# Small pads that move the start addresses of TensorE's operands, in a hybrid decoder block on one core

## The chip, the cores and the metric

The kernel runs on one core of one Trainium2 chip. A core has a matrix engine (TensorE, PE in the profile, which reads two operands from the on-chip memory SBUF: the moving one, streamed through the array, and the stationary one, the weights, which a separate load puts into the array), VectorE (DVE), ScalarE (ACT), GpSimd (POOL) and a queue engine (SP) that issues most transfers. SBUF has 128 partitions; a tile takes the same range of bytes in each of them, and a start address here is the byte in that range. The metric is device microseconds (us) of one execution, lower is better, as the median of several runs.

## The reference

One decoder layer over 512 tokens of width 2048, all in float32:

```python
mod = jax.nn.silu(c) @ w_ada[l] + b_ada[l]
sh1, sc1, ga1, sh2, sc2, ga2 = jnp.split(mod, 6, axis=-1)
h = modulate(rmsnorm(x, g_mix_norm[l]), sh1, sc1)
proj = h @ w_in[l]
...
y_ssm = s5_mixer(u, ...)            # diagonal complex state space, 64 groups of 16 channels
y_att = nsa_mixer(q, kc, vc, ks, vs, kw, vw, gl, ...)   # 16 heads, 4 key/value heads
y = jnp.concatenate([rmsnorm(y_ssm, g_ssm_out[l]), rmsnorm(y_att, g_nsa_out[l])], axis=-1) @ w_out[l]
x = x + ga1[:, None, :] * y
h = modulate(rmsnorm(x, g_ffn_norm[l]), sh2, sc2)
x = x + ga2[:, None, :] * conv_ffn(h, w_up[l], conv_w[l], conv_b[l], w_down[l])
return rmsnorm(x, g_final)
```

`conv_ffn` multiplies by `w_up` (2048 x 11264), runs a causal convolution of width 3 over each channel, gates one half with the silu of the other and multiplies by `w_down` (5632 x 2048).

## The kernel before, in words

Every large product keeps float32 precision by three passes (`mm3`, lines 87 to 89): each operand is split into a high part (a cast, on ACT) and a low part (the rest, a subtraction on DVE; both on line 62), and the product is hi x hi, then hi x lo, then lo x hi, summed in one PSUM tile. In the names, `wh` and `wl` are high and low part of a piece of weights and `ah`/`al`, `yh`/`yl`, `hh`/`hl`, `b11h`/`b11l` those of the activations. The three matmuls of a step thus alternate between two moving operands and two stationary ones. In a name of the trace such as `dn<-ah,wh`, `dn` is the result, `ah` the moving operand and `wh` the stationary one.

The program runs in stages, each with its pools of tiles:

- `phase_a` and `phase_b1` (to about 520 us): the input projections (results `b` and `mm`, operands `hh`, `hl`, 512 columns) and the state-space part `s5_octet`, in 8 octets.
- `phase_b2` (to about 860 us): attention, with the gated unit `glu` and half of the output projection as filler (`mm<-yh`).
- `phase_c` (to about 975 us): the other half of the output projection (`mm<-yh` again), with the modulation weights `wada` streamed in.
- `up_first` and `up_rest` (to about 1875 us): the product with `w_up`. `up_first` does two columns of tiles plainly, `up_rest` the other 42 (`c` = 2 to 43) by Strassen's scheme in Winograd's form: seven products of 24 matmuls of 256 columns each per `c` (8 steps of `mm3`), each with its own moving operand, in this order on PE: `b11`, `t4`, `b21`, `t1`, `t2`, `b22`, `t3` (a part of `t4` stands ahead of `b21`, the rest behind it). The weights of the products alternate between two pairs of tiles by a counter over all products (`turn`): `wh`, `wl` of the pool `wp`, and `xh`, `xl` of the pool `pe`. Seven is odd, so a product that reads `wh` in one `c` reads `xh` in the next one.
- `down` (to the end): the product with `w_down` (result `dn`, moving `ah`, `al`, stationary `wh`, `wl`, 512 columns; the last quarter in halves of 256, partly from a further weight tile `wz`), then the final norm.

Pools take SBUF from two ends: a pool is stacked on the left or, with `side="right"`, on the right, in steps of 32 bytes, and a tile's start follows from the sizes of everything below it in its stack. `cp` (small vectors and constants) and then `wp` (the weights' buffers `wr`, `wh`, `wl`) are at the bottom on the left for the whole program. Above them come the pools of the stages; `ta` (the taps of the convolution) goes in after `phase_b1` and stays. On the right stand `sc` (a vector `silc`), `pg` (`yh`, `yl`, `yatt`, `z`), later `pt` (the operands `b11` to `t3` of `up_rest`), later `pr` (`ah`, `al`).

Of the kernel before, what the change touches and what calls it, by code (L numbers as in the profile page):

```python
# [10 lines left out]
F32 = mybir.dt.float32  # L11
# [7 lines left out]
P = 128  # L19
# [5 lines left out]
NFF = D_FF // P  # L25
# [14 lines left out]
NV = 168  # L40

C_ID, C_T31, C_INVD, C_INVH, C_INVH4, C_SGN, C_NSGN, C_GRP, C_CHN, C_COS, C_SIN = (
    0, 192, 193, 194, 195, 196, 197, 198, 206, 334, 846)
# [8 lines left out]
class Block:  # L52
# [88 lines left out]
    def setup(self):  # L141
        nc, tc, a, ctx = self.nc, self.tc, self.a, self.ctx
        self.cp = ctx.enter_context(tc.tile_pool(name="cp", bufs=1))
        self.wp = ctx.enter_context(tc.tile_pool(name="wp", bufs=1))
        self.dp = ctx.enter_context(tc.tile_pool(name="dp", bufs=1, space=DRAM))
        cp = self.cp
        self.vecs = cp.tile([P, NV], F32, name="vecs")
        self.cons = cp.tile([P, C_COS], F32, name="cons")
        self.ident = self.cons[:, C_ID:C_ID + P]
        self.mhalf = cp.tile([P, 1], F32, name="mhalf")  # L150
        nc.vector.memset(self.mhalf, -0.5)
        self.mod = cp.tile([P, 6, KT], F32, name="mod")
        self.mad = cp.tile([P, 6, KT], F32, name="mad")
        d = self.dp

        self.u_d = d.tile([8, 8, P, 64], F32, name="u_d")

        self.z_d = d.tile([8, P, 8, 64], F32, name="z_d")

        self.k_s = d.tile([8, 16, 15 * P], F32, name="k_s")  # L160

        self.qk_d = d.tile([3, HD * 8, 2, S], F32, name="qk_d")

        self.c_d = d.tile([2, 2 * P, S], F32, name="c_d")
        self.sh_d = d.tile([1, D], F32, name="sh_d")
        self.x_d = d.tile([P, KT, S], F32, name="x_d")
        self.x2_d = d.tile([P, KT, S], F32, name="x2_d")

        self.a_d = d.tile([P, NFF, S], F32, name="a_d")
        self.v_d = d.tile([4, P, S], F32, name="v_d")  # L170
# [319 lines left out]
    def s5_octet(self, o, Tb, W, ps):  # L490
# [3 lines left out]
        G = slice(g0, g0 + 8)  # L494
        hp = self.tc.high_priority
        U, bc = self.s5_next
        SS = W.tile([P, 8, 65], F32, name="s5SS")
        V.memset(SS[:, :, 0:1], 0.0)
        bx, cx = bc[:, 0], bc[:, 1]

# [124 lines left out]
        V.tensor_mul(z5, z3, Sf)  # L625
        V.tensor_add(SS[:, :, 1:65], z4.rearrange("p (g j) -> p g j", g=8), z5.rearrange("p (g j) -> p g j", g=8))
        with hp():
            Y = ps.tile([P, S], F32, name="acc", bufs=4)
            for g in range(8):
                T.matmul(Y[:, 64 * g:64 * g + 64], w3[:, :, g], U[:, g], start=True, stop=False)  # L630
                T.matmul(Y[:, 64 * g:64 * g + 64], TT[:, g, 0:8].rearrange("p k h -> p (k h)"), SS[:, g, 0:64],
                         start=False, stop=True)
# [677 lines left out]
    def run(self):  # L1310
        tc = self.tc
        self.setup()
        sc = ExitStack()
        self.silc = sc.enter_context(tc.tile_pool(name="sc", bufs=1, side="right")).tile([P, D], F32, name="silc")
        lt = ExitStack()
        with tc.tile_pool(name="ph", bufs=1) as ph:
            hh, hl = map(list, zip(*[[ph.tile([P, S], F32R, name=f"h{x}{k}") for x in "hl"] for k in range(KT)]))
            with tc.tile_pool(name="psa", bufs=1, space=PSUM) as ps:
                self.phase_a(hh, hl, ph, ps)
            self.late(lt.enter_context(tc.tile_pool(name="pk", bufs=1, reuse_waits="tile", side="right")))  # L1320
            self.phase_b1(hh, hl)
        ta = self.ctx.enter_context(tc.tile_pool(name="ta", bufs=1, reuse_waits="tile"))
        self.taps = ta.tile([P, 88, 4], F32, name="taps")
        self.tapn = ta.tile([P, NFF, 3], F32, name="tapn")
        with ExitStack() as st:
            with ExitStack() as sg:
                pg = self.pg = sg.enter_context(tc.tile_pool(name="pg", bufs=1, reuse_waits="tile", side="right"))
                ps = sg.enter_context(tc.tile_pool(name="psd", bufs=1, reuse_waits="tile", space=PSUM))
                self.acc_att = pg.tile([P, S], F32, name="acc_att")
                self.acc_ssm = pg.tile([P, S], F32, name="acc_ssm")  # L1330
                self.rba = [pg.tile([P, 256], F32, name=f"rba{i}") for i in range(2)]
                yatt = pg.tile([P, 8, S], F32, name="yatt")
                yh = pg.tile([P, 8, S], F32R, name="yh")
                yl = pg.tile([P, 8, S], F32R, name="yl")
                self.phase_b2(yatt, yh, yl, ps)
                px = st.enter_context(tc.tile_pool(name="px", bufs=1, reuse_waits="tile"))
                x2 = [px.tile([P, 4, S], F32, name=f"x2{q}") for q in range(4)]
                self.acc2 = px.tile([P, S], F32, name="acc2")
                self.rb2 = px.tile([P, S], F32, name="rb2")
                W = st.enter_context(tc.tile_pool(name="py", bufs=1, reuse_waits="tile"))  # L1340
                with tc.tile_pool(name="pz", bufs=1, reuse_waits="tile") as Wa:
                    self.phase_c(x2, yatt, yh, yl, W, Wa, ps)
            lt.close()
            sc.close()
            self.phase_d(x2, W, st)
# [143 lines left out]
```

## Time and profile before

| | us |
|---|---|
| median of three runs | 2400.34 |
| the three runs | 2392.76, 2400.34, 2401.52 |
| the profiled execution, whole | 2398.66 |
| its span, first to last instruction | 2396.9 |
| PE busy in it | 2244.6 (94%) |
| DVE busy | 1865.8 (78%) |
| ACT busy | 1084.3 (45%) |

The span is 1.8 us shorter than the profiled execution's own time, which is 1.7 us under the median. Busy is the time in which at least one instruction of the engine was under way. Matmuls overlap: one that takes 0.28 us from its start to its end may be followed by the next 0.11 us after its start. How fast PE works is therefore read from the distance between starts of matmuls in the timeline, not from busy time or durations.

### The profile page before, as it was taken

What the parts mean: (1) busy time and instruction counts of PE and PEld (TensorE: products, weight loads), DVE (VectorE), ACT (ScalarE), POOL (GpSimd) and SP (SyncE); (2) the same over time, 40 slices, a digit from 0 to 9 for tenths busy, and PEclk for the clock granted to TensorE, in tenths of its full rate; (3) what the DMA queues carried; (4) which work ended last, traced back from release to release, by engine and by line L of the source; (5) the groups of instructions that cost most, each with busy time, mean ns of one, the idle gap of its engine ahead of it and who ended that gap; (6) DMA issues with size and microseconds to landing.
All of it is one profiled execution on the core that took longest, in us unless ns stands there. A gap on an engine that the chain in (4) does not pass through costs nothing.

```text
span 2396.9 us, 34691 instructions
## 1 busy us (share of the span) xinstructions
PE 2244.6 (94%) x13694; PEld 1967.3 (82%) x13694; DVE 1865.8 (78%) x2776; ACT 1084.3 (45%) x1807; POOL 288.5 (12%) x375
## 2 busy tenths in 40 slices
PE   7778999989899879899999999999999899999997
PEld 5666787866677667889999999999999788888887
DVE  7789877749988878889999999999999685433436
ACT  3322444448867742644444444444444322221215
POOL 7996110100000011000000000000000000000000
PEclk9989998979999889999999999999999999999999
DMA  9666744676576567233333333333332684323223
GB/s 339 255 223 215 235 146 140 186 207 195 174 233 218 186 251 289 101 120 119 119 119 119 119 119 119 120 119 119 119 119 102 243 322 182 139 90 126 101 88 106
DMA packets 92370, 398.17 MB, mean 166 GB/s; under 512 B 19776, under 2 KB 28352, under 8 KB 56240
## 3 DMA queue, kind: packets, MB, share of 16 engines
q1 hardware_dynamic: 77856, 344.60, 41.6%
q0 software_dynamic: 14352, 51.36, 6.1%
q8 instruction: 107, 1.75, 0.3%
q14 instruction: 55, 0.45, 0.1%
HBM read 358.20 MB, written 37.69 MB: 165 GB/s over the span
## 4 chain that ended last, share of the span: by engine, by line
PE 71%; DVE 11%; issue 6%; POOL 5%; ACT 4%; DMA 3%; SPq 0%; POOLq 0%; DVEq 0%; ACTq 0%
PE dn L88 7%; PE dn L87 7%; PE dn L89 7%; PE sa L89 7%; PE sa L87 7%; PE sa L88 7%; PE sb L87 5%; PE sb L89 5%; PE sb L88 5%; PE mm L87 2%; PE mm L89 2%; PE mm L88 2%; DVE wl L62 2%; DVE adw L111 1%; PE s L870 1%
## 5 line engine op out<-in xcount | busy, mean ns | idle before, releaser
L62 ACT CAST wh<-wr 128x1024 fp32r<-128x1024 f32 (+1 forms) x257 | 261.9, 1024 | 519.7 <-PE dn L88 331.6
L62 DVE TENSOR_TENSOR wl<-wr,wh 128x1024 fp32r<-128x1024 f32 (+1 forms) x255 | 307.2, 1209 | 68.6 <-ACT wh L62 47.7
L87 PE MATMUL dn<-ah,wh 128*128 128x512 f32 (+1 forms) x704 | 274.9, 391 | 7.6 <-ACT ah L62 7.6
L88 PE MATMUL dn<-al,wh 128*128 128x512 f32 (+1 forms) x704 | 278.0, 395 | 0.0
L89 PE MATMUL dn<-ah,wl 128*128 128x512 f32 (+1 forms) x704 | 273.3, 388 | 0.0
L1249 DVE SCALAR_TENSOR_TENSOR x<-dn,mod,x 128x512 f32<-128x512 f32 (+1 forms) x104 | 73.2, 707 | 203.4 <-PE dn L89 202.8
L87 PEld LDWEIGHTS dn<-ah,wh 128*128 128x128 f32 x704 | 132.8, 189 | 40.8 <-ACT ah L62 7.8
L89 PEld LDWEIGHTS dn<-ah,wl 128*128 128x128 f32 x704 | 132.7, 189 | 30.3
L111 DVE SCALAR_TENSOR_TENSOR adw<-adw,silc 128x2048 f32<-128x2048 f32 x63 | 147.9, 2348 | 12.1 <-DMA adw<-in_wada_dram 11.8
L88 PEld LDWEIGHTS dn<-al,wh 128*128 128x128 f32 x704 | 132.8, 189 | 29.6 <-DVE al L62 0.4
L87 PE MATMUL mm<-yh,wh 128*128 128x512 f32 (+1 forms) x320 | 130.4, 412 | 22.5 <-DVE x L1026 7.2
L62 ACT CAST wh<-wq 128x1024 fp32r<-128x1024 f32 x84 | 88.0, 1048 | 137.6 <-DVE wq L1193 101.0
L62 ACT CAST xh<-wq 128x1024 fp32r<-128x1024 f32 x84 | 88.5, 1054 | 135.8 <-DVE wq L1193 100.8
L88 PE MATMUL mm<-yl,wh 128*128 128x512 f32 (+1 forms) x320 | 129.7, 406 | 3.9 <-DVE yl L62 3.9
L1082 POOL DMA_DIRECT2D a_d<-cv x44 | 23.9, 543 | 879.4 <-DVE cv L1081 879.4
L89 PE MATMUL mm<-yh,wl 128*128 128x512 f32 (+1 forms) x320 | 129.1, 405 | 0.3 <-DVE wl L62 0.3
L62 DVE TENSOR_TENSOR wl<-wq,wh 128x1024 fp32r<-128x1024 f32 x84 | 102.4, 1220 | 33.1 <-ACT wh L62 33.1
L62 DVE TENSOR_TENSOR xl<-wq,xh 128x1024 fp32r<-128x1024 f32 x84 | 102.5, 1220 | 31.4 <-ACT xh L62 31.4
L1193 DVE TENSOR_TENSOR wq<-wq,wr 128x1024 f32<-128x1024 f32 x84 | 102.1, 1216 | 0.1
L87 PEld LDWEIGHTS mm<-yh,wh 128*128 128x128 f32 x320 | 63.0, 199 | 37.7 <-issue 12.3
L87 PE MATMUL b<-hh,wh 128*128 128x512 f32 x192 | 67.3, 408 | 23.6 <-ACT hh L238 16.4
L62 ACT CAST xh<-wr 128x1024 fp32r<-128x1024 f32 x63 | 65.8, 1044 | 47.0 <-issue 19.9
(525 smaller groups left out, 7207.3 us busy)
## 6 DMA issues: line engine op xcount, KB each, us to landing
adw<-in_wada_dram SPq DMA_DIRECT2D x49, 1024.0 KB, 7.0
wr<-in_wup_dram SPq DMA_DIRECT2D x46, 1024.0 KB, 4.9
wq<-in_wup_dram SPq DMA_DIRECT2D x42, 1024.0 KB, 6.6
wr<-in_wdn_dram SPq DMA_DIRECT2D x40, 1024.0 KB, 4.9
wr<-in_wada_dram SPq DMA_DIRECT2D x32, 1024.0 KB, 4.9
wr<-in_wout_dram SPq DMA_DIRECT2D x16, 1024.0 KB, 5.8
adw<-in_wada_dram POOLq DMA_DIRECT2D x14, 1024.0 KB, 6.9
wr<-in_wp_dram SPq DMA_DIRECT2D x12, 1024.0 KB, 5.6
```

The lines of the kernel that those rows point to most:

```text
L62: return self.A.copy(hi, src), self.V.tensor_sub(lo, src, hi.bitcast(F32))
L87: self.T.matmul(ps, wh, xh, start=start, stop=False)
L88: self.T.matmul(ps, wh, xl, start=False, stop=False)
L89: self.T.matmul(ps, wl, xh, start=False, stop=stop)
L111: self.V.scalar_tensor_tensor(t, t, 1.0, self.silc, op0=ALU.mult, op1=ALU.mult, accum_out=out)
L870: T.matmul(s[:, :c + n], q[hd], K[b][:, i, k0:k0 + c + n], start=i == 0, stop=i == 1)
L1082: self.nc.gpsimd.dma_start(self.a_d[:, m], val)
L1193: V.tensor_add(src, src, add)
L1249: V.scalar_tensor_tensor(x, p, self.mod[:, 5, m:m + 1], x, op0=ALU.mult, op1=ALU.add)
```

## The change

Five tiles get a few floats more than they use, one is declared wider and used in part, and one pad tile of 8 floats (32 bytes) is put at the bottom of the right stack. No operation is added or removed, and the shapes that the engines work on stay the same; only the row of `s5SS` grows from 65 to 66 floats.

```diff
-        self.vecs = cp.tile([P, NV], F32, name="vecs")
-        self.cons = cp.tile([P, C_COS], F32, name="cons")
+
+        self.vecs = cp.tile([P, 176], F32, name="vecs")[:, 0:NV]
+        self.cons = cp.tile([P, 336], F32, name="cons")
...
-        self.mhalf = cp.tile([P, 1], F32, name="mhalf")
+        self.mhalf = cp.tile([P, 16], F32, name="mhalf")[:, 0:1]
...
-        SS = W.tile([P, 8, 65], F32, name="s5SS")
+        SS = W.tile([P, 8, 66], F32, name="s5SS")
...
         self.setup()
+        self.ctx.enter_context(tc.tile_pool(name="rp", bufs=1, side="right")).tile([P, 8], F32, name="pad")
...
-        self.tapn = ta.tile([P, NFF, 3], F32, name="tapn")
+        self.tapn = ta.tile([P, NFF + 4, 3], F32, name="tapn")[:, 0:NFF]
```

`NV` is 168, `C_COS` 334 and `NFF` 44. In bytes `vecs` was 672, which is 32 more than a multiple of 64, and `tapn` was 528 (544 in steps of 32), again 32 more; `vecs`, `cons` and `mhalf` together came to a multiple of 64, so that `wp` above them started at one and `cons` itself did not. The start of a tile, in bytes past a multiple of 64, in the two programs:

| tiles | read by PE as | before | after |
|---|---|---|---|
| `wr`, `wh`, `wl` (all stages) | stationary | 0 | 0 |
| `hh`, `hl` (`phase_a`, `phase_b1`) | moving, 512 columns | 0 | 0 |
| `yh`, `yl` (`phase_b2`, `phase_c`) | moving, 512 or 256 | 32 | 0 |
| `Q`, `K`, `Vs`, `th`, `tl`, `Pt`, `cons` | both | 32 | 0 |
| tiles of `s5_octet` but `s5U` (0) | both | 32 | 0 |
| `b11` to `t3` (`up_first`, `up_rest`) | moving, 256 | 32 | 0 |
| `rh`, `rl` (`up_first`), `xh`, `xl` (`up_rest`) | stationary | 32 | 0 |
| `ah`, `al` (`down`) | moving, 512 or 256 | 32 | 0 |
| `wz` (end of `down`) | stationary | 32 | 0 |

The slices of these tiles that the large products read are multiples of 512 bytes apart, so that the table holds for them too. Taken past a multiple of 512 bytes the starts are: before, `hh` and `wh` 384 both, `b11` to `t3` and `ah` 480, `yh` 224, `xh` 288; after, `hh`, `wh`, `b11` to `t3` and `ah` 448 all, `yh` 192, `xh` 384.

The engines' lists of instructions are the same in both programs, row for row, and so are their waits, with one exception: on ACT the first cast `yh<-z` of `phase_b2` (line 62) also waits for a transfer `k_s<-s5bg` of the octet before the last one, since its tile now begins 32 bytes lower and the source of that transfer ends 96 bytes higher, so that their places overlap by 128 bytes where they only touched before.

## Rows read from the trace of the kernel before

**Rows 1.** Busy time per engine, part 1 of the page.
```profile
PE 2244.6 (94%) x13694; PEld 1967.3 (82%) x13694; DVE 1865.8 (78%) x2776; ACT 1084.3 (45%) x1807; POOL 288.5 (12%) x375
```

**Rows 2.** Windows: stretch, us, busy of PE, PEld, DVE, ACT, POOL; PEclk; DMA.
```profile
540.00:860.00 320.00, 286.95 (x1389) 217.22 (x1388) 281.97 (x767) 247.52 (x649) 12.56 (x18) 0.94 0.60 195
860.00:1030.00 170.00, 146.42 (x860) 128.77 (x860) 138.86 (x213) 73.42 (x129) 20.15 (x35) 0.92 0.59 218
1030.00:1875.00 845.00, 839.25 (x7053) 830.33 (x7052) 766.94 (x840) 406.02 (x466) 23.36 (x43) 1.00 0.33 118
1875.00:2397.00 522.00, 501.27 (x2245) 407.40 (x2244) 265.79 (x330) 145.18 (x185) 1.95 (x3) 0.98 0.44 158
```

**Rows 3.** Timeline of PE in phase_a: start, duration (us), line; 27 starts apart.
```profile
61.79 0.39 PE L87 MATMUL b<-hh,wh 128*128 128x512 f32 x1
...
67.91 0.39 PE L87 MATMUL b<-hh,wh 128*128 128x512 f32 x1
```

**Rows 4.** Timeline of PE in phase_c, 69 starts apart.
```profile
893.14 0.39 PE L87 MATMUL mm<-yh,wh 128*128 128x512 f32 x1
...
909.24 0.39 PE L87 MATMUL mm<-yh,wh 128*128 128x512 f32 x1
```

**Rows 5.** Timeline of PE in down, 42 starts apart.
```profile
1980.16 0.39 PE L87 MATMUL dn<-ah,wh 128*128 128x512 f32 x1
...
1989.96 0.39 PE L87 MATMUL dn<-ah,wh 128*128 128x512 f32 x1
```

**Rows 6.** Timeline of PE in up_rest: the first matmul of each product.
```profile
1082.10 0.28 PE L87 MATMUL sa<-t4h,wh 128*128 128x256 f32 x1
...
1088.05 0.28 PE L87 MATMUL sa<-t1h,xh 128*128 128x256 f32 x1
...
1090.80 0.28 PE L87 MATMUL sb<-t2h,wh 128*128 128x256 f32 x1
...
1093.67 0.28 PE L87 MATMUL sa<-b22h,xh 128*128 128x256 f32 x1
...
1096.40 0.28 PE L87 MATMUL sa<-t3h,wh 128*128 128x256 f32 x1
...
1099.27 0.28 PE L87 MATMUL sb<-b11h,xh 128*128 128x256 f32 x1
...
1101.99 0.28 PE L87 MATMUL sa<-t4h,xh 128*128 128x256 f32 x1
...
1107.95 0.29 PE L87 MATMUL sa<-t1h,wh 128*128 128x256 f32 x1
...
1110.83 0.28 PE L87 MATMUL sb<-t2h,xh 128*128 128x256 f32 x1
```

**Rows 7.** Tile t3h in up_rest: durations in ns, min/median/max.
```profile
L87 PE MATMUL sa<-t3h,wh x168: 279/282/286, 1056.5 to 1857.0; 128*128 128x256 f32 x168
...
L87 PE MATMUL sa<-t3h,xh x160: 276/276/276, 1076.5 to 1837.0; 128*128 128x256 f32 x160
```

**Rows 8.** Lines by form, PE: busy us, mean ns, idle before, releaser.
```profile
L87 PE MATMUL dn<-ah,wh 128*128 128x512 f32 x672 | 265.7, 396 | 7.6 <-ACT ah L62 7.6
L87 PE MATMUL mm<-yh,wh 128*128 128x512 f32 x288 | 121.5, 424 | 19.8 <-DVE x L1026 7.2 <-ACT wh L62 3.9 <-DVE mod L318 3.8
```

**Rows 9.** Lines of DVE in up_rest: busy us, mean ns, idle before.
```profile
L62 DVE TENSOR_TENSOR xl<-wq,xh 128x1024 fp32r<-128x1024 f32 x84 | 102.5, 1220 | 31.4 <-ACT xh L62 31.4
...
L62 DVE TENSOR_TENSOR wl<-wr,wh 128x1024 fp32r<-128x1024 f32 x62 | 75.7, 1221 | 1.8 <-ACT wh L62 0.3
```

**Rows 10.** Waits in up_rest: waiter, releaser, us in total, times, longest us.
```profile
ACT wh L62 <- PE sa L88: 74.7, 41, 1.8
...
PEld sb L87 <- ACT p L1201: 8.2, 41, 0.2
```

**Rows 11.** Tile k_s: issues on POOL, ns, first and last start.
```profile
L581 POOL DMA_DIRECT2D k_s<-s5bg x2: 508/508/508, 447.1 to 474.9; - x2
```

**Rows 12.** Tile yh at the start of phase_b2, the same columns.
```profile
L62 ACT CAST yh<-z x8: 601/610/615, 519.9 to 539.3; 128x512 fp32r<-128x512 f32 x8
```

## The prediction, made before the changed kernel was timed

> **What bounds the kernel now.** I read the page's busy times first: PE is busy for 94% of the span, the next engine for 78% [rows 1]. Busy time does not say how fast PE works, so I then cut the span into its stages [rows 2]. [...]
>
> The third view is the timeline of PE alone, read for the distance from start to start of equal matmuls in stretches without a wait. It shows two speeds, and they go with the start addresses:
>
> - `phase_a`, 512 columns, moving and stationary operand both at 0 past a multiple of 64 bytes: 27 starts in 67.91 - 61.79 = 6.12 us, 226.7 ns each [rows 3].
> - `phase_c`, 512 columns, moving at 32, stationary at 0: 69 starts in 16.10 us, 233.3 ns [rows 4].
> - `down`, the same pairing: 42 starts in 9.80 us, 233.3 ns [rows 5].
> - `up_rest`, 256 columns, moving always at 32, stationary at 0 (`wh`) or 32 (`xh`) in turn. A product is 24 matmuls. With `xh` it takes 2.75 (`t1`), 2.73 (`b22`) and 2.72 us (`b11`), with `wh` 2.87 (`t2`), 2.87 (`t3`) and 2.88 us (`t1`) [rows 6]. That is 113.9 ns against 119.7 ns per matmul.
>
> So it is not the address of one operand that costs: moving and stationary both at 32 run as fast per column (113.9 for 256) as both at 0 (226.7 for 512). It costs when the two differ by 32. `t3` shows it without other differences: the same moving tile, the same shape, and durations of 276/276/276 ns with `xh` against 279/282/286 with `wh` [rows 7]. After the change every one of these pairs stands at 0 and 0, so I expect the fast distance everywhere.
>
> [...]
>
> **The sum, against the profiled execution** (2398.66 us).
>
> 1. `up_rest`: 42 values of `c`, so each of the seven products reads `wh` in 21 of them and `xh` in 21. For `t1`, `t2`, `b22`, `t3`, `b11` the gain is 2.873 - 2.733 = 0.14 us for each of 5 x 21 = 105 products: 14.7 us. `t4` and `b21` stand interleaved behind a wait of PE for the copy of `p` on ACT (8.2 us in 41 times [rows 10]); the two take 5.95 us with `t4` on `wh` and 5.96 us with `t4` on `xh` [rows 6]. Two undisturbed products on `xh` would be 5.47 us, so 0.5 us is wait and what follows it. The copy has to end in any case; a faster start of `t4` only arrives earlier at it. The bounds for these 42 blocks are no gain and the full 0.14 us of the one product in each that reads `wh`, 5.9 us; I take the middle, 2.9. Together 17.6 us.
> 2. `down`: 672 steps of three matmuls of 512 columns on `wh`, `wl` [rows 8]; each matmul goes from 233.3 to 226.7 ns: 672 x 3 x 6.6 = 13.3 us. The last quarter has 32 steps of 256 columns on `wh` at 3 x 5.8 ns: 0.6 us. Those on `wz` are in step already and stay.
> 3. `up_first`: 64 steps on `wh` (two `c`, two halves, two results, 8 steps), 256 columns: 64 x 3 x 5.8 ns = 1.1 us.
> 4. `phase_b2` and `phase_c`: 288 steps of `mm<-yh` of 512 columns [rows 8], 5.7 us at 3 x 6.6 ns, and 64 of 256 columns, 1.1 us. PE is not always what ends last there: `wada` weights, the splits on ACT and the softmax on DVE have waits of their own, and part of these steps runs at the lower clock. The bounds are nothing and 6.8 us; I take 3.0, somewhat under half.
> 5. `phase_a`, `phase_b1`: already at 0 and 0; nothing. The attention and state-space matmuls were at 32 and 32; nothing. Also nothing for the row of `s5SS`, whose eight additions and 64 small matmuls keep their shapes.
>
> What else moves is hidden or unmoved. DVE does not mind the residue: the same subtraction takes 1220 ns on tiles all at 32 and 1221 ns on tiles all at 0 [rows 9]. The added wait of ACT asks for a transfer issued at 474.9 us, 45 us before the cast that waits at 519.9 [rows 11, 12]; without that cover it would cost, once, what was left of that transfer. The pads are written by nobody.
>
> Behind a faster PE, DVE is next in `up_rest`. It needs 767 of 845 us, 91%. With 17.6 us less the stage lasts 827 us and DVE is at 93%. ACT's casts there wait for PE to free their buffers (74.7 us for one tile's alone [rows 10]), so the splits run ahead and their lead is not used up.
>
> Sum: 17.6 + 13.9 + 1.1 + 3.0 = 35.6 us; by the bounds of steps 1 and 4 it is 29.7 to 42.3. The profiled execution would be 2363.1 us. It stands 1.7 us under the median of the runs; from that median I get 2400.3 - 35.6 = 2364.7, called **2365 us**, with 2358 to 2371 by the bounds. The three runs lie 8.8 us apart, so a median can sit a few us off; the forecast's own range is 2354 to 2375.
>
> **Rivals.**
>
> - *No effect*, 2400 us. The two speeds could belong to the tiles `xh` and `wh` (their place, or the buffers' traffic) and not to the difference of 32. [...] Against it: `wh` itself runs at 226.7 with `hh` and 233.3 with `yh` [rows 3, 4]. 0.06.
> - *Only a part*. Either the lead of the splits goes, and DVE, at 91%, eats the gain of `up_rest`: 18.0 us are left, 2382 us. Or a further bit of the address counts: then `wh`, now at no distance from `b11` to `t3`, gains 20.6 us at most, and `xh`, which goes from 192 to 64 bytes below them, loses as much; with `down` and the rest again 2382. `hh` and `wh` show that no distance at all is fine [rows 3]; 64 bytes no row shows. 0.10 for both.
> - *Slower*: the same further bit, but against both. `xh` falls out of step (147 products by 0.14 us, 20.6 us lost) and the products on `wh`, and `down`, stay as they are: 2421 us. It decides from the point where more products leave the fast distance than enter it; in the trace that needs the starts of `xh` products to move from 2.73 to 2.87 us. Nothing shows it. 0.04.
>
> The forecast itself has 0.80.
>
> **Numbers.** A difference under 0.5% (12 us) is about what a measurement of this kernel cannot tell from none. The forecast and the partial case both lie beyond it (16 us and more), so faster is 0.80 + 0.10 less a little for a partial case that ends smaller, 0.89; same 0.07; slower 0.04. The range goes from the forecast's lower end, 2354, to the partial case, 2383.
>
> **What would show it.** In the profile after: products of `up_rest` all at 2.72 to 2.75 us, `t3h,wh` at a median duration of 276 ns, `dn` at 226.7 ns from start to start, and the stage of `up_rest` some 18 us shorter with DVE's busy time unchanged. `phase_a` and `phase_b1` keep their length. I am wrong if `wh` products stay at 2.87 us (no effect), if `xh` products rise (a further bit), or if PE gains idle time behind splits on DVE in `up_rest` (DVE is next).

## The result, and the profile after

The changed kernel takes 2377.58 us (median of six runs, 2370.02 to 2383.45), the kernel before 2395.91 on the same chips (2388.89 to 2401.52): a ratio of 0.993, 95% interval 0.9912 to 0.9947. That is faster, by 18.3 us where 35.6 were forecast.

The profiled execution of the changed kernel takes 2375.8 us with a span of 2374.0, 22.9 less than before. Its busy times, part 1 of the page, answer to [rows 1]:

```profile
PE 2223.8 (94%) x13694; PEld 1963.5 (83%) x13694; DVE 1864.5 (79%) x2776; ACT 1083.3 (46%) x1807; POOL 284.5 (12%) x375
```

PE is busy for 20.8 us less, the other engines differ by 4 or less. Where it comes from shows in the lengths of the stages, each read in the timeline of PE from the first product of one stage to the first of the next one (in us; `phase_b2` ends with the last product of the attention, and 1.1 us less stand ahead of the first product):

| | `phase_a` | `phase_b1` | `phase_b2` | `phase_c` | `up_first` | `up_rest` | `down` | norm |
|---|---|---|---|---|---|---|---|---|
| before | 225.7 | 281.6 | 339.1 | 123.1 | 49.7 | 852.5 | 497.2 | 14.8 |
| after | 227.3 | 276.6 | 339.5 | 120.2 | 49.7 | 850.3 | 483.1 | 15.1 |
| forecast of the difference | 0 | 0 | -3.0 with `phase_c` | | -1.1 | -17.6 | -13.9 | 0 |

`down` gave what was forecast, `up_rest` almost nothing. The 5.0 us of `phase_b1` show no cause in the addresses and are put down to scatter: the operands of its large products are at no distance from each other in every kernel of this study, and in the five other kernels below that run the whole computation, four of them with the left stack as changed, it takes 278.0 to 282.8 us. `phase_b2` (334.2 to 341.1 us over all seven kernels) and `phase_c` (119.3 to 124.8) scatter as much, so their small differences say little.

The timeline of PE in `down` (start, duration), 30 starts apart, answers to [rows 5]: 6.80 us, 226.7 ns from start to start where it was 233.3.

```profile
1980.23 0.39 PE L87 MATMUL dn<-ah,wh 128*128 128x512 f32 x1
...
1987.03 0.39 PE L87 MATMUL dn<-ah,wh 128*128 128x512 f32 x1
```

The same of `phase_c`, 69 starts apart, answers to [rows 4]: 15.64 us, again 226.7 ns.

```profile
892.41 0.39 PE L87 MATMUL mm<-yh,wh 128*128 128x512 f32 x1
...
908.05 0.39 PE L87 MATMUL mm<-yh,wh 128*128 128x512 f32 x1
```

The timeline of PE in `up_rest`, the first matmul of each product, answers to [rows 6]:

```profile
1080.78 0.28 PE L87 MATMUL sa<-t1h,xh 128*128 128x256 f32 x1
...
1083.50 0.28 PE L87 MATMUL sb<-t2h,wh 128*128 128x256 f32 x1
...
1086.38 0.28 PE L87 MATMUL sa<-b22h,xh 128*128 128x256 f32 x1
...
1089.10 0.28 PE L87 MATMUL sa<-t3h,wh 128*128 128x256 f32 x1
...
1091.98 0.28 PE L87 MATMUL sb<-b11h,xh 128*128 128x256 f32 x1
...
1094.70 0.28 PE L87 MATMUL sa<-t4h,xh 128*128 128x256 f32 x1
...
1100.57 0.28 PE L87 MATMUL sa<-t1h,wh 128*128 128x256 f32 x1
```

A product of 24 matmuls on `xh` takes 2.72 us (113.3 ns each), one on `wh` still 2.88 (120.0 ns), about as before. And tile `t3h` (duration in ns, min/median/max, first and last start) has kept the two durations of [rows 7]:

```profile
L87 PE MATMUL sa<-t3h,wh x168: 282/283/283, 1049.4 to 1848.0; 128*128 128x256 f32 x168
...
L87 PE MATMUL sa<-t3h,xh x168: 276/276/276, 1069.3 to 1867.8; 128*128 128x256 f32 x168
```

So 512 columns against weights at the same residue became fast, and 256 columns against weights at the same residue did not. In what follows the **distance** of a pair is the start of its moving operand less the start of its stationary one, past a multiple of 256 bytes. From the starts given ahead of the prediction it is, before: 96 for `wh` and 192 for `xh` in `up_rest`, 96 in `phase_c` and `down`, 0 in `phase_a`. After: 0 for `wh` and 64 for `xh` in `up_rest`, 0 in the other three.

### The profile page after: what moved, and what is told of

It is laid out like the page before. It is cut to its first block, busy times and chain, and to the rows that moved or that the text cites. A ratio compares the mean times of both kernels' runs of the same rounds, so it can differ in the third digit from the quotient of the medians.

```text
span 2374.0 us, 34691 instructions
## 1 busy us (share of the span) xinstructions
PE 2223.8 (94%) x13694; PEld 1963.5 (83%) x13694; DVE 1864.5 (79%) x2776; ACT 1083.3 (46%) x1807; POOL 284.5 (12%) x375
## 4 chain that ended last, share of the span: by engine, by line
PE 71%; DVE 10%; issue 6%; POOL 5%; ACT 4%; DMA 3%; SPq 0%; POOLq 0%; DVEq 0%; ACTq 0%
PE dn L88 7%; PE dn L87 7%; PE dn L89 7%; PE sa L89 7%; PE sa L88 7%; PE sa L87 7%; PE sb L87 5%; PE sb L89 5%; PE sb L88 5%; PE mm L87 2%; PE mm L89 2%; PE mm L88 2%; POOL stt L339 2%; DVE wl L62 2%; PE s L871 1%
## 5 line engine op out<-in xcount | busy, mean ns | idle before, releaser
L88 PE MATMUL dn<-al,wh 128*128 128x512 f32 (+1 forms) x704 | 271.3, 386 | 0.0
```

Source lines behind the costliest of these rows:

```text
L88: self.T.matmul(ps, wh, xl, start=False, stop=False)
```

## The experiments

**Every distance by itself.** The whole computation is left out. What remains is a loop of 96 matmuls in each section, against two 128x128 pieces of weights in turn, which start 512 bytes apart and stay where they are; the moving start goes up by 32 bytes from section to section, for 256 (`ea` to `ep`), 512 (`fa` to `fp`) and 128 columns (`ga` to `gp`).

```diff
+    for n, head in ((256, "e"), (512, "f"), (128, "g")):
+        for i in range(16):
...
+                for m in range(NMM):
+                    o = 8 * i + 512 * (m % 8)
+                    T.matmul(p[:, 0:n], ws[:, m % 2], xm[:, o:o + n], start=m == 0, stop=m == NMM - 1)
```

> This kernel leaves the whole computation out: it measures the disputed cost by itself. One pair of weight slices at a fixed place (128 bytes past a multiple of 512) and a moving tile; 48 sections of 96 matmuls each, 256 columns (results ea to ep), then 512 (fa to fp), then 128 (ga to gp), and from section to section the moving operand starts 32 bytes further: distance moving minus weights 0, 32, 64, ... 480. Theory A (the distance counts, with a period of 128 bytes): at 256 columns 113.3 ns from start to start where the distance is 64, 192, 320 or 448, and 120 ns elsewhere; at 512 columns 226.7 ns at 0, 128, 256, 384, and 231 to 238 at distances of 32 and 96 more; 64 past a multiple of 128 no run has shown at 512 columns: 220 ns if each matmul loses one step of 6.7 ns more at the wrong distance, 226.7 if only equality past a multiple of 64 counts there. Theory B (the place or the traffic of the buffer wh makes its products slow at 256 columns, and the distance counts only past a multiple of 64): 113.3 and 226.7 ns at all eight multiples of 64.

The timeline of this kernel from the first settled matmuls of a section to its last one; a row is start, time to the end of the last, and the count:

```profile
13.71 9.05 PE L76 MATMUL ea<-xm,ws 128*128 128x256 f32 x74
...
37.91 8.88 PE L76 MATMUL ec<-xm,ws 128*128 128x256 f32 x74
50.04 9.04 PE L76 MATMUL ed<-xm,ws 128*128 128x256 f32 x74
86.69 8.55 PE L76 MATMUL eg<-xm,ws 128*128 128x256 f32 x74
135.33 7.87 PE L76 MATMUL ek<-xm,ws 128*128 128x256 f32 x68
209.76 16.71 PE L76 MATMUL fa<-xm,ws 128*128 128x512 f32 x73
255.98 16.87 PE L76 MATMUL fc<-xm,ws 128*128 128x512 f32 x73
279.05 17.20 PE L76 MATMUL fd<-xm,ws 128*128 128x512 f32 x73
```

Less the length of one matmul (0.28 or 0.39 us) and divided by the count less one, `ea` (distance 0) gives 120 ns, `eg` (192) 113.3, and 64 bytes 117.8 in `ec` but 113.3 in `ek`; `fa` (0) 226.7, `fd` (96) 233.5. All sections read in this way, by single starts, in ns:

| distance | 0 | 32 | 64 | 96 | 128 | 160 | 192 | 224 |
|---|---|---|---|---|---|---|---|---|
| 256 columns | 120.0 | 116.7 | 117.8 or 113.3 | 120.0 | 120.0 | 118.7 | 113.3 | 118.3 |
| 512 columns | 226.7 | 233.3 | 228.9 | 233.3 | 233.4 | 234.3 | 233.3 | 233.3 |
| 128 columns | 111.6 | 111.7 | 111.6 | 111.7 | 111.6 | 111.7 | 111.6 | 111.7 |

The sections from 256 bytes on repeat the first eight within 0.1 ns, but for one: 256 columns at 64 bytes ran at 117.8 ns in its first section and at 113.3 in its second. So the period is 256 bytes, and neither theory that was written down holds: one took 128 bytes for the period, the other any multiple of 64 for equal. The best distance is another one for each count of columns: 0 is among the three slowest for 256 columns and the fastest for 512. The readings of both kernels lie in this table: before 119.7 (96) and 113.9 (192) in `up_rest` and 233.3 (96) in `down`; after 120.0 (0), 113.3 (64) and 226.7 (0).

**The right pad alone**, on the kernel before. The tiles of the right stack go to multiples of 64 bytes, so `wh` is in step with them as in the changed kernel, while `xh` falls out of step. Distances: 64 for `wh`, 160 for `xh`, 64 in `down`.

```diff
         self.setup()
+        self.ctx.enter_context(tc.tile_pool(name="rp", bufs=1, side="right")).tile([P, 8], F32, name="pad")
```

> The kernel before with the pad of 8 floats on the right stack alone: b11 to t3, ah and yh move down by 32 bytes, nothing else moves. Distance moving minus weights past a multiple of 128: 64 for wh in up_rest and down, 32 for xh, 64 for yh with wh. Theory A: products on wh go from 2.87 to 2.73 us, those on xh from 2.73 to 2.87, up_rest unchanged within 2 us; down gains 13 us (226.7 ns per matmul of 512 columns) or 27 us (220 ns); in all 13 to 30 us under the kernel before, 2366 to 2383. Theory B: products on wh stay at 2.87, those on xh rise to 2.87, up_rest 18 to 20 us longer, down 13 us shorter: 2 to 8 us over the kernel before.

It takes 2388.17 us, the kernel before beside it 2395.78: 0.9971 (0.9951 to 0.999). Tile `t3h` of this kernel:

```profile
L87 PE MATMUL sa<-t3h,wh x168: 279/280/281, 1052.3 to 1856.3; 128*128 128x256 f32 x168
...
L87 PE MATMUL sa<-t3h,xh x160: 277/281/283, 1072.3 to 1836.4; 128*128 128x256 f32 x160
```

Neither outcome that was written down came: one had 2366 to 2383 us, the other 2 to 8 us over the kernel before. By starts, `wh` runs at 117.7 and `xh` at 118.0 ns (table: 117.8 and 118.7); `up_rest` takes 857.4 us, `down` 487.7. From the changed kernel's 483.1 `down` is 4.6 us off, over 2016 matmuls 2.3 ns each: 229.0, the table's 228.9 for 64. A pair that is equal past a multiple of 64 bytes is thus neither at 226.7 nor at 233.3.

**All at multiples of 64, at other distances.** The changed kernel with the right pad at 96 bytes instead of 32. Everything still starts at a multiple of 64. Distances: 192 for `wh`, 0 for `xh`, 192 in `down`.

```diff
-        self.ctx.enter_context(tc.tile_pool(name="rp", bufs=1, side="right")).tile([P, 8], F32, name="pad")
+        self.ctx.enter_context(tc.tile_pool(name="rp", bufs=1, side="right")).tile([P, 24], F32, name="pad")
```

> The changed kernel with a right pad of 24 floats in place of 8: everything on the right moves down by a further 64 bytes, all tiles stay at multiples of 64. Distance past a multiple of 128: wh with b11 to t3 and with ah 64 (was 0), xh 0 (was 64). Theory A: wh products 2.73 us, xh products 2.88, so up_rest as in the changed kernel within 2 us; down as in the changed kernel, or 13 us shorter still if 512 columns run at 220 ns at this distance. Theory B: nothing changes anywhere against the changed kernel, wh stays at 2.88 and xh at 2.73.

It takes 2402.70 us, a ratio of 1.0032 to the kernel before (1.0018 to 1.0045): the whole gain is gone, and a little more. Tile `t3h` of this kernel, and its windows of `up_rest` and `down` (stretch, us, busy of PE, PEld, DVE, ACT, POOL, granted clock, DMA share and GB/s):

```profile
L87 PE MATMUL sa<-t3h,wh x168: 280/281/282, 1053.5 to 1862.7; 128*128 128x256 f32 x168
...
L87 PE MATMUL sa<-t3h,xh x160: 282/283/284, 1073.6 to 1842.5; 128*128 128x256 f32 x160
```

```profile
1029.00:1890.70 861.70, 849.25 (x7057) 840.58 (x7057) 772.66 (x848) 408.71 (x468) 23.10 (x44) 1.00 0.32 118
1890.70:2387.10 496.40, 496.33 (x2216) 403.97 (x2216) 252.74 (x310) 140.22 (x177) 1.11 (x2) 1.00 0.42 155
```

Now it is `xh` that is at distance 0 and has the 283 ns that `wh` had, 120.0 from start to start; `wh` runs at 117.9, `down` at 233.3 in 496.4 us. The 120.0 ns follow the distance, not the tile, and a multiple of 64 bytes is no rule at all. Both theories of the text above miss here, since each expected the gain to stay, and the table by itself misses too: `wh` is at 192 and should run at 113.3 ns. It has the 117.8 ns that 64 bytes showed as a second speed, so 192 has a second speed as well.

**The change without its right pad.** The left stack as changed, the right stack as before. Distances: 32 for `wh`, 96 for `xh`, 32 in `phase_c` and `down`.

```diff
-        self.ctx.enter_context(tc.tile_pool(name="rp", bufs=1, side="right")).tile([P, 8], F32, name="pad")
```

> The changed kernel without the pad at the bottom of the right stack: all else at multiples of 64 bytes, but the tiles of the right stack (yh, b11 to t3, ah) stay at 32 past one. Distances past 256 bytes: wh 32, xh 96 in up_rest, 32 in down and in phase_c. Theory A, by the kernel of all distances: 116.65 ns on wh (3.0 better than before), 120.0 on xh (6.4 worse), 233.3 in down as before: up_rest 852.5 - 10.6 + 22.6 = 864 us, down 497, the whole 2395.9 + 12 = 2408 us. Theory of the change (only equality past a multiple of 64 counts): both pairs out of step, wh stays at 119.7, xh goes from 113.9 to 119.7: 852.5 + 20.5 = 873 us, the whole 2416 us. No effect of addresses: 2396 us.

It takes 2405.15 us, 1.0041 times the kernel before beside it (2394.53; 1.002 to 1.0063), near the 2408 that the table gives and not the 2416 of the theory of the change. The same two views:

```profile
L87 PE MATMUL sa<-t3h,wh x168: 277/279/281, 1058.9 to 1867.0; 128*128 128x256 f32 x168
...
L87 PE MATMUL sa<-t3h,xh x160: 281/283/285, 1079.0 to 1846.9; 128*128 128x256 f32 x160
```

```profile
1034.60:1895.20 860.60, 848.06 (x7056) 839.14 (x7056) 772.27 (x847) 409.96 (x468) 23.34 (x44) 1.00 0.33 118
1895.20:2392.00 496.80, 496.67 (x2216) 403.00 (x2216) 252.73 (x310) 140.40 (x177) 0.97 (x2) 1.00 0.43 154
```

By starts `wh` is at 116.8 and `xh` at 119.9 ns, so two pairs that are equally out of step past 64 bytes run at different speeds. The halves of the change do not add up: the right pad alone gains 7.6 us, the rest alone loses 10.6, and the two together gain 18.3.

**Both pairs of `up_rest` at 192 bytes.** The changed kernel with three more pads of 64 bytes, one below the operands `b11` to `t3` on the right, one below the tiles of `up_rest` and one below those of `phase_b2`/`phase_c` on the left. `up_rest` has distance 192 throughout, the products of 512 columns keep 0. The instructions and their order are those of the changed kernel; a few transfers wait for other semaphores.

```diff
+            sd.enter_context(tc.tile_pool(name="pu", bufs=1, side="right")).tile([P, 16], F32, name="padr")
             R = sd.enter_context(tc.tile_pool(name="pt", bufs=1, reuse_waits="tile", side="right"))
...
         with tc.tile_pool(name="pe", bufs=1, reuse_waits="tile") as W:
+            W.tile([P, 16], F32, name="padx")
...
+                st.enter_context(tc.tile_pool(name="pv", bufs=1)).tile([P, 16], F32, name="padw")
                 W = st.enter_context(tc.tile_pool(name="py", bufs=1, reuse_waits="tile"))
```

> The changed kernel with three more pads of 64 bytes: in up_rest the moving tiles now start 192 bytes (taken past a multiple of 256) from both pairs of weight tiles, wh and xh; down and the output projection keep a distance of 0. Theory A (what counts is the distance of the two starts past a multiple of 256 bytes, with the table that the kernel of all distances gave: 120.0 ns at 0, 113.3 at 64 and 192, for 256 columns): the products on wh go from 120.0 to 113.3 ns a matmul, 147 products x 24 x 6.7 ns = 23.6 us, less what the wait for the copy of p takes back (up to 6), so up_rest falls from 850.3 to 827 to 833 us and the whole from 2377.6 to 2354 to 2360 us; down stays at 483. Theory A with a lock: 64 and 192 have a second steady speed of 117.8 ns into which a stretch may fall and stay; if both pairs fall into it, wh gains 7.8 us and xh loses 15.7, the whole is 2385 us. Theory C (VectorE, busy for nine tenths of the stage, takes over as the bound): matmuls at 113.3 ns, but up_rest not under 843 us, PE idle behind the splits, the whole about 2370 us. Theory of the change (equal past a multiple of 64 bytes is enough, the rest was the buffers' traffic): no change, 2378 us.

It takes 2356.58 us (2353.89 to 2358.97), 0.9848 times the kernel before (0.9832 to 0.9864), within the 2354 to 2360 of theory A, and so beats both: the intervals of this kernel and of the changed one do not meet. Tile `t3h`, and the windows of `up_rest` and `down`:

```profile
L87 PE MATMUL sa<-t3h,wh x168: 276/276/276, 1054.3 to 1830.0; 128*128 128x256 f32 x168
...
L87 PE MATMUL sa<-t3h,xh x168: 276/276/276, 1073.6 to 1849.3; 128*128 128x256 f32 x168
```

```profile
1030.00:1857.30 827.30, 814.63 (x7056) 805.68 (x7056) 768.61 (x848) 406.47 (x468) 23.56 (x44) 0.99 0.34 123
1857.30:2340.70 483.40, 483.33 (x2216) 403.20 (x2216) 251.81 (x309) 140.05 (x177) 0.97 (x2) 1.00 0.44 159
```

Every product but the two interleaved ones runs at 113.3 ns. `up_rest` is 827.3 us, 23.0 less than in the changed kernel, and `down` keeps its 483. DVE is busy for 768.6 of 827.3 us, 93%, and does not become the bound; PE's waits in the stage are (waiter, releaser, us, times, longest)

```profile
PE sb L87 <- ACT p L1204: 3.9, 1, 3.9
PE sb L89 <- DVE wl L62: 0.8, 1, 0.8
PE sb L89 <- DVE xl L62: 0.2, 1, 0.2
```

once each, 1.0 us in all for splits on DVE. The weight loads ahead of PE wait 1.5 us for splits and 12.5 us, in 42 times, for the copy of `p`; in the changed kernel it is 1.5 and 12.1. The interleaved `t4` and `b21` give their share too. Timeline, from the start of `t4` to that of `t1`, 48 matmuls:

```profile
1117.72 0.28 PE L87 MATMUL sa<-t4h,wh 128*128 128x256 f32 x1
...
1123.45 0.28 PE L87 MATMUL sa<-t1h,xh 128*128 128x256 f32 x1
```

5.73 us, where the changed kernel has 5.87 with `t4` on `xh` (in the rows of its `up_rest` above), and the kernel before 5.95 and 5.96 [rows 6]; over all `c` the kernel before has 5.88 or 5.95 with `t4` on `wh` and 5.96 with it on `xh`.

**Both pairs at 64 bytes.** The same three pads, but with 192 bytes in the one below `b11` to `t3`.

```diff
-            sd.enter_context(tc.tile_pool(name="pu", bufs=1, side="right")).tile([P, 16], F32, name="padr")
+            sd.enter_context(tc.tile_pool(name="pu", bufs=1, side="right")).tile([P, 48], F32, name="padr")
```

> As the kernel with 192 bytes, but with the moving tiles of up_rest 64 bytes (past a multiple of 256) from both pairs of weight tiles. Theory A: 64 is the mirror of 192, so the same 113.3 ns and 2354 to 2360 us. Theory A with a lock: the changed kernel fell into the slower speed (117.5 ns) at 64 bytes only in products that follow a stall of PE, and the kernel of all distances did so in its first section at 64; if here, where no product comes from the 120 ns of distance 0, nearly all products run at 117.5 to 117.8, up_rest is 850.3 - 7.8 + 15 = 857 to 859 us and the whole 2385 us. Theory of the change: 2378 us.

It takes 2372.21 us (0.9915; 0.9893 to 0.9937), between the two outcomes that were written down; `up_rest` takes 846.4 us. Timeline of PE, the first matmuls of three products in one `c` and in the next one:

```profile
1129.86 0.28 PE L87 MATMUL sb<-t2h,wh 128*128 128x256 f32 x1
...
1132.68 0.28 PE L87 MATMUL sa<-b22h,xh 128*128 128x256 f32 x1
...
1135.51 0.28 PE L87 MATMUL sa<-t3h,wh 128*128 128x256 f32 x1
...
1149.60 0.28 PE L87 MATMUL sb<-t2h,xh 128*128 128x256 f32 x1
...
1152.32 0.28 PE L87 MATMUL sa<-b22h,wh 128*128 128x256 f32 x1
...
1155.04 0.28 PE L87 MATMUL sa<-t3h,xh 128*128 128x256 f32 x1
```

In the first `c` a product takes 2.82 to 2.83 us (117.8 ns), in the next one 2.72 (113.3). Read product by product, all from `b21` of one `c` to `t4` of the next one have the same speed, and it changes only at the stall where PE waits for the copy of `p`: the fast one in 14 of 42, the slow one in 28. At 64 bytes there are two speeds that keep themselves up until the next stall; with both pairs at 192 all 42 went into the fast one.

**What chooses between the two.** Again the computation is left out: a bare loop with 48 matmuls at one distance, and then, without a gap, 96 at another (in the first section, 0 and then 64, four of each stand ahead of the rest).

```diff
+    for n, d1, d2 in ENTRY:
...
+            for p, d, cnt in zip(pair, (d1, d2), (48, NMM)):
+                for m in range(cnt):
+                    o = d // 4 + 512 * (m % 8)
+                    T.matmul(p[:, 0:n], ws[:, m % 2], xm[:, o:o + n], start=m == 0, stop=m == cnt - 1)
```

> The whole computation is left out; a bare loop of matmuls, 128x128 weights in two slices in turn, in sections of two parts without a gap: 48 matmuls with the moving start at one distance from the weights, then 96 at another. Question: is the second speed at 64 and 192 bytes, 256 columns, chosen by what ran before? If by the history: 64 entered from 0 (120.0 ns) runs at 113.3 and 192 entered from 0 at 117.8; 192 entered from 96 at 113.3; and the two differ by the part before. If by chance: no order among the twelve sections. If the speeds are fixed by the distance alone: 113.3 in all twelve. Finer distances: theory A with a bank or line of 64 bytes or more lets 8, 16 and 24 bytes run like 0 or between 0 and 32 (226.7 to 233.3 ns at 512 columns); a grain of 32 bytes makes 8 to 24 all equal to 0 and 40 to 56 all equal to 32; if every byte counts, all differ.

Timeline of this kernel, settled matmuls, in this order: 64 bytes entered from 0, 32 from a standing start, 192 entered from 0, 32 from a standing start again, 192 entered from 64.

```profile
17.80 9.58 PE L79 MATMUL v<-xm,ws 128*128 128x256 f32 x80
...
28.24 5.53 PE L79 MATMUL u<-xm,ws 128*128 128x256 f32 x46
...
124.01 9.34 PE L79 MATMUL v<-xm,ws 128*128 128x256 f32 x81
...
135.39 4.40 PE L79 MATMUL u<-xm,ws 128*128 128x256 f32 x36
...
193.12 10.06 PE L79 MATMUL v<-xm,ws 128*128 128x256 f32 x84
```

That is 117.7, 116.7, 113.3, 117.7 and 117.8 ns. In all, 192 runs at 113.3 from a standing start and after 0, 32, 96, 160 and 192, and at 117.8 after 64; 64 runs at 117.8 in all six sections. So history counts, as the last row shows, and a second section that goes from 64 to 192 repeats it. But the expected order by history failed on both counts: 64 entered from 0 did not reach 113.3 here, though in the changed kernel the products on `xh` (64), each right behind one on `wh` (0), nearly all do; and 192 entered from 0 did, though in the kernel with 96 bytes of pad the products on `wh` (192), each right behind one on `xh` (0), run at 117.9. What picks the speed at 64 and 192 bytes stays open. Nor are the other distances all of one speed: 32 ran at 116.7 and at 117.7 from a standing start, and 160 at 117.2 and 117.3, where the table has 118.7. Of the finer distances, at 512 columns: 8 bytes 233.3, 16 bytes 231.7, 24 bytes 232.4, 40 bytes 234.1, 48 bytes 230.0, 56 bytes 233.4. None runs like 0 (226.7), and they differ among themselves; nothing smaller than 8 bytes was tried. At 256 columns 48 and 80 bytes gave 118.3, and 56, 72, 184 and 200 bytes 120.0. So the fast distances are narrow: 8 bytes beside 64 or 192 a matmul already takes as long as at 0.

## Why the prediction was right or wrong

The direction was right and the time lies in the range, but 12.6 us from the figure, and it got there by the wrong sum: one of its two large terms came out in full and the other one hardly at all. That the range holds the time is luck: the forecast's own range ended at 2375 us, and the part above it was put there for a rival.

- **Step 1, `up_rest`, failed:** 17.6 us forecast, 2.2 measured. The sentence that broke is "After the change every one of these pairs stands at 0 and 0, so I expect the fast distance everywhere", and with it the remark against the rival of a further bit, that `hh` and `wh` "show that no distance at all is fine [rows 3]". That row is of 512 columns. At 256 columns no distance is among the worst cases, 120.0 ns, no better than the 119.7 before. The rows ahead of the prediction held two fast pairs, 0 at 512 columns and 192 at 256, and the step took what they share past 64 bytes, where both are 0, for the cause. The kernel with 96 bytes of pad, which keeps that and loses the gain, shows that it is not.
- **What happened instead** is the second half of the rival "only a part": a further bit of the address counts. Its 2382 us was near by luck, since its reasons were others. It let `wh` gain 20.6 us and `xh` lose as much; in fact neither moved, since `wh` went from one slow distance to another (96 to 0, 119.7 to 120.0 ns) and `xh` from one fast one to another (192 to 64, 113.9 to 113.3 ns in nearly all products).
- **The size of step 1 was right for the right cause.** With both pairs at 192 bytes `up_rest` loses 23.0 us against the changed kernel and 25.2 against the kernel before. That is more than the 17.6, since `t4` and `b21`, put at 2.9 us, give more: 5.88 to 5.96 us there against 5.73, summed over the 42 values of `c` 8.5 us. The other 105 products on `wh` go from 2.87 to 2.72 us, some 16 us, and the two make nearly all of the 25.
- **Step 2, `down`, held:** 13.9 forecast, 14.1 measured, 226.7 ns from start to start: 2016 matmuls at 6.6 ns less are 13.3 us, so here the time taken from each matmul came off the stage in full. Its 0.6 us for the 32 steps of 256 columns rests on the failed assumption; the table gives them nothing at distance 0.
- **Step 3, `up_first`,** 1.1 us forecast, 0.0 measured: 256 columns at distance 0 on `wh`, the same failure in small.
- **Step 4, `phase_b2` and `phase_c`,** 3.0 forecast, 2.5 measured (0.4 lost, 2.9 gained). The agreement shows little: in `phase_c` the settled matmuls of 512 columns went from 233.3 to 226.7 ns, but the stage also took 119.3 us in the kernel without the right pad, where they are at distance 32.
- **Step 5:** `phase_a` is 1.6 us longer, `phase_b1` 5.0 shorter, both without a cause that shows in the addresses; that scatter can make up the difference between the 22.9 us of the profiled execution and the 18.3 of the medians. The added wait of ACT stayed hidden: the cast that got it starts at 515.47 us without a gap behind the one before.
- **The other rivals.** No effect at all is refuted by the bare loop: the same instructions take 113.3 or 120.0 ns when only the moving start changes and the weights stay where they are. Whether it is the weight loads that cost the running matmul, no run shows, as none leaves them out. DVE as the next bound is refuted up to the 93% that the prediction had worked out, by the kernel that reached it. The slower case exists: two of the experiments, the changed kernel without its right pad and with a larger one, take 0.4% and 0.3% more than the kernel before.

## What to carry to other kernels

Where matmuls with weight loads between them follow each other without a wait, read the distance from start to start per pair of tiles and set it beside the distance of their starts past 256 bytes, the period that the bare loop showed here; a bare loop over the distances, for each count of columns in use, costs one run and is worth more than any rule read from two pairs. Alignment by itself is no target (with every start at a multiple of 64 bytes the kernel took 2377.58 us with one right pad and 2402.70 with another): choose the distance per pair (here 0 for 512 columns, 226.7 ns, and 192 for 256, 113.3), judge all pads together, since each shifts everything above it in its stack, and read the speed again in the kernel itself: beside a pair at distance 0 the pair at 192 ran at 117.9 ns, not at 113.3. When rows of one shape seem to settle a rule for another, find a row of that shape first.

## What the runs showed of the hardware

- In the bare loop, with 96 weight loads for the 96 matmuls of a section and a granted clock of 0.993 over the whole run (1.00 in two stretches of 8 us at 256 columns), the start distance of moving and stationary operand changes a matmul's pace: 113.3 to 120.0 ns at 256 columns, 226.7 to 234.3 at 512, nothing at 128 (111.6 to 111.7). The distances from 256 to 480 bytes repeat those from 0 to 224 within 0.1 ns, but for 64 bytes at 256 columns (117.8 and 113.3), so the period is 256 bytes. A step of 8 bytes off the fast distance already costs 6.6 ns at 512 columns (226.7 at 0, 233.3 at 8 bytes) and 6.7 at 256 (113.3 at 192, 120.0 at 184 and at 200).
- At 256 columns two steady speeds exist at 64 and at 192 bytes, 113.3 and 117.8 ns. With both pairs of the stage at 64 bytes a stretch kept the one it had until the next stall, the fast one in 14 of 42 and the slow one in 28; at 192 bytes the slow one was met only behind 64 in the bare loop (117.8 ns) and, in the kernel with 96 bytes of pad, behind products at distance 0 (117.9 ns). What chooses between them stays open.
- Why a matmul is slower at some distances, whether the weight loads are what gets in its way, and why 0 is best for 512 columns (226.7 ns) and among the worst for 256 (120.0), no run here shows.
